# Mirror sums and differences, a narrower band and split pool weights in a two-layer mixer on one core

## The chip, the cores and the metric

The kernel runs on one core of one Trainium2 chip. The metric is the device time of one execution in microseconds (us), as a median of several runs. TensorE (PE) multiplies matrices, VectorE (DVE) and ScalarE (ACT) work on elements, SyncE (SP) issues the DMAs; GpSimd (POOL) does next to nothing here. Each engine takes its instructions in one fixed order. A matmul result lies in PSUM, everything else in SBUF.

## The reference

256 latent and 256 context tokens of width 2048 pass through two layers. In each layer one input projection feeds three mixers: attention, a mean over windows minus the token itself ("pool"), and the real part of a 2-D Fourier transform. The mixers' outputs are concatenated, multiplied by a gate and projected back. The last layer needs only keys and values of the context.

```
def multiscale_pool(u, pool_w, pool_scale):        # windows 2, 4, 8, 16, one for each of 4 groups
    ...
        outs.append(win_sum / cnt[None, :, None] - uf[:, :, gi])
    y = jnp.einsum('bngc,gcd->bngd', pooled, pool_w).reshape(B, N, POOL_W)
    return y * pool_scale

def fourier_mix(u, fourier_w):                     # 4 groups of 128 channels
    ...
    f = jnp.fft.fft2(uf, axes=(1, 3), norm='ortho').real.astype(u.dtype)
    return jnp.einsum('bngc,gcd->bngd', f, fourier_w).reshape(B, N, FOURIER_W)

def reference(...):
    for l in range(DEPTH):
        shift, scale, gate = jnp.split(jax.nn.silu(c) @ ada_w[l] + ada_b[l], 3, axis=-1)
        h = rmsnorm(x, norm_g[l]) * (1.0 + scale[:, None]) + shift[:, None]
        q, k, v, up, uf, g = split_proj(h @ w_in[l])
        ...
        out = merge_branches(att, up, uf, g, pool_w[l], pool_scale[l], fourier_w[l], w_out[l])
        x_new = x + gate[:, None] * out
        ...  # the same for the context tokens, except in the last layer
    return rmsnorm(x, final_norm_g)
```

## The kernel before

**Products in two parts.** Nearly every product is kept near full precision by splitting both operands into a high and a low part, each of a reduced type (fp32r). `mm3` (L336 to L338) issues three matmuls: high by high, high by low, low by high. `split` makes the parts: ScalarE copies with rounding to the high part (L138), DVE subtracts that from the source for the low part (L139).

**Weights.** `wpiece` loads 128x1024 pieces (`raw`) and splits them into `whi` and `wlo`, with three buffers of each. They are used once, so ScalarE and DVE split each weight piece of the kernel while PE multiplies the piece before.

**Stages of a layer.** `b_chunk` computes 512 columns of the input projection for all tokens: 4 token tiles of 128 in layer 0 (latent and context), 2 in layer 1 (latent). Chunk 0 holds the pool channels, chunk 1 the Fourier channels, chunk 2 the keys and values. Then follow gates, queries, attention and the output projection. After chunks 0 and 1, `evac_tok` splits the token-major result into high and low parts (`u`).

**Pool branch.** For each of four groups a first product with a band matrix of 256x256 (L359, token tile by token tile) gives z, which ScalarE copies to SBUF (L364). The second product with the 128x128 pool weights is one matmul of full-precision operands (L347), and DVE writes it scaled (L349).

**Fourier branch.** The channel transform and the Fourier weights are folded into one table `fh`, `fl` per layer (L404, L406, L407). For each group the first product multiplies both token tiles of a sequence by 256 columns of cosines and sines (`dh`, `dl`): six matmuls per sequence. z is split by `split`, and the second product multiplies it by `fh`, `fl`, 130 columns for the cosine half and 128 for the sine half. DVE writes the mirror halves of the output as sum and difference (L428, L429).

**What sets the order.** Branches are generators. While PE runs a chunk, `side.tick(0.64)` advances a clock, and a branch takes its next step when the clock passes what it asked for (`yield`, in us, and a lag). LAG_E and the numbers at the yields thus decide between which weight products a step's matmuls stand. `fill(n)` adds n units of adaLN work for later stages: one 512 KB load (`araw`) and two products on DVE with an accumulated sum (`ajunk`, L189) against a broadcast of c (`cbt`). The broadcast has one buffer, reloaded when the unit list passes to another half of c. These units have low priority, weights and evacuations a high one (AHEAD). A scheduler then puts each engine's instructions into one order, in which they wait for each other.

**PSUM.** Chunk results use four tiles (`mm`), the branches four others (`sm`).

Of the kernel before, what the change touches and what calls it, by code (L numbers as in the profile page):

```python
# [28 lines left out]
WINDOWS = (2, 4, 8, 16)  # L29

# [15 lines left out]
LEAD = 3  # L46
LAG_S, LAG_T, LAG_E, LAG_Q = 4.3, 1.4, 5.6, 0.0
# [3 lines left out]
FILL = ((1.69, 1.5, 0.55, 1.43, 1.0), (0.04, 1.61, 0.01, 0.66, 0))  # L51
# [4 lines left out]
def backbone(  # L56
# [270 lines left out]

    def pair8(n, rest):
        q8 = late["q8"]
        if n == 4:  # L330
            return [q8.tile([P, n, *rest], F32R, tag="q8", name=name("q8")) for _ in range(2)]
        t = q8.tile([P, 2, n, *rest], F32R, tag="q8", name=name("q8"))
        return t[:, 0], t[:, 1]
# [6 lines left out]
    def pool_branch(l, u, mixed, off, nst):  # L340
# [4 lines left out]
        def second(g, zs):  # L345
            y = smt()
            PE.matmul(y[:, :nt], pwt[:, g], zs, start=True, stop=True)  # L347
            for s in range(nst):
                V.scalar_tensor_tensor(  # L349
                    mixed[2][:, g, off + s * N : off + s * N + N], y[:, s * N : s * N + N], psc[:, l * 4 + g : l * 4 + g + 1], it[:, g],  # L350
                    op0=ALU.mult, op1=ALU.mult,
                )

        for g in range(4):
            z = smt()
            for s in range(nst):
                for mt in range(2):
                    for i in range(2):
                        PE.matmul(  # L359
                            z[:, s * N : s * N + N], u[i][:, 2 * s + mt, g * P : g * P + P], br[g][:, mt],  # L360
                            start=mt == 0 and i == 0, stop=mt == 1 and i == 1,
                        )
            zs = t2("z", (P, nt))
            S.copy(zs, z[:, :nt])  # L364
# [10 lines left out]
    def pool_tables(l):  # L375
        pwt = t2("pw", (P, 4, P))
        nc.sync.dma_start(pwt, pw[l])
        it = f4("icnt", (P, 4, N), F32)
# [9 lines left out]
        tabs.update(p=(pwt, it, br))  # L388
# [21 lines left out]
    def fourier_branch(l, u, mixed, off, nst):  # L410
# [20 lines left out]
        for g in range(4):  # L431
            c = slice(g * P, g * P + P)
            z = smt()
            for s in range(nst):
                for mt in range(2):
                    mm3(z[:, s * N : s * N + N], u[0][:, 2 * s + mt, c], u[1][:, 2 * s + mt, c], dh[:, mt], dl[:, mt], mt == 0, mt == 1)
            zh, zl = t2("zh", (P, 512), F32R), t2("zl", (P, 512), F32R)
            split(z[:, :nt], zh[:, :nt], zl[:, :nt])
            yield 0.72 * nst, 1.3
# [131 lines left out]
    def layer(l, h, xs, chunk0):  # L571
# [35 lines left out]
        u = evac_tok(accs, ntt)  # L607
# [4 lines left out]
        side.add("four", fourier_branch(l, u, mixed, off, nst), LAG_E)  # L612
# [437 lines left out]
def _order():  # L1050
    h = N // 2
    return np.concatenate([np.arange(h + 1), N - np.arange(1, h)])


def _tables():
# [12 lines left out]
    ang = 2 * np.pi * (np.outer(t, t) % N) / N  # L1068
    d = np.concatenate([np.cos(ang), np.sin(ang)], 1).astype(np.float32)
    dft = d.reshape(2, P, 512).transpose(1, 0, 2)  # L1070
    dft0 = np.concatenate([dft[:, :, : N // 2 + 1], dft[:, :, N + 1 : N + N // 2]], 2)
# [80 lines left out]
```

## Time and profile before

| | us |
|---|---|
| median of 3 runs (1077.66 to 1080.66) | 1078.14 |
| profiled execution | 1079.1 |
| its span in the trace | 1077.2 |
| PE busy | 1045.6 |
| DVE busy | 846.3 |
| ACT busy | 480.5 |

The conditioning for layer 0 is made first, from large loads; from then on PE has work nearly throughout. Matmuls are pipelined: the duration of one in the trace overlaps the next, so what a matmul costs is read from start to start. DVE's rows are shorter from start to start than they are long, too. A row with a bracket says how long the engine was idle before it, and what ended that.

### The profile page before, as it was taken

The numbers are of one execution on the slowest core, as the hardware profiler recorded it, in microseconds if no ns is written. First come the engines' busy times: TensorE is split into PE (matmuls) and PEld (weight loads), VectorE is DVE, ScalarE is ACT, GpSimd is POOL, SyncE is SP. The second block draws the span as 40 slices with busy tenths as digits, with TensorE's granted clock in tenths as the row PEclk, the third lists the DMA queues.
The fourth block names the chain that finished last, engine by engine and source line by source line (L and its number), as shares of the span: only waits on it lengthen the run. The fifth ranks groups of instructions, "written<-read, shape, count | busy, mean of one in ns | idle before, by whom it ended". The sixth has DMA issues, their size and how long they took to land.

```text
span 1077.2 us, 14001 instructions
## 1 busy us (share of the span) xinstructions
PE 1045.6 (97%) x5065; PEld 842.2 (78%) x5065; DVE 846.3 (79%) x1566; ACT 480.5 (45%) x807; POOL 0.2 (0%) x4
## 2 busy tenths in 40 slices
PE   5999899999999999999999999999999999999996
PEld 3466577788787888888888888888888888888885
DVE  6458656998999879997999887589656888776564
ACT  5233234323413765642532223288326768547443
POOL 0000000000000000000000000000000000000000
PEclk9999999999999999999999999999999999999998
DMA  9999857457685334457786657435765565776563
GB/s 355 414 368 345 277 200 239 157 190 233 200 266 195 96 122 155 157 195 259 251 286 218 198 195 262 139 127 190 246 229 170 159 195 184 236 262 215 180 213 115
DMA packets 64133, 234.15 MB, mean 217 GB/s; under 512 B 7153, under 2 KB 8257, under 8 KB 60353
## 3 DMA queue, kind: packets, MB, share of 16 engines
q1 hardware_dynamic: 64064, 233.28, 63.4%
q8 instruction: 39, 0.64, 0.3%
q14 instruction: 30, 0.24, 0.1%
HBM read 231.12 MB, written 2.12 MB: 217 GB/s over the span
## 4 chain that ended last, share of the span: by engine, by line
PE 66%; DVE 6%; issue 3%; ACT 1%; DMA 1%; ACTq 0%; SPq 0%; DVEq 0%
PE mm L336 17%; PE mm L338 17%; PE mm L337 17%; PE mm L312 5%; DVE ajunk L189 3%; PE mm L313 2%; PE sm L337 2%; PE sm L336 2%; PE sm L338 2%; DVE wlo L139 1%; PE sm L557 1%; DMA cbt<-cd 1%; PE sm L520 1%; DMA araw<-in_adar 0%; ACT whi L138 0%
## 5 line engine op out<-in xcount | busy, mean ns | idle before, releaser
L138 ACT CAST whi<-raw 128x1024 fp32r<-128x1024 f32 (+1 forms) x216 | 219.9, 1019 | 333.5 <-PE mm L338 108.5
L139 DVE TENSOR_TENSOR wlo<-raw,whi 128x1024 fp32r<-128x1024 f32 (+1 forms) x216 | 255.1, 1182 | 104.4 <-ACT whi L138 103.2
L189 DVE SCALAR_TENSOR_TENSOR ajunk<-araw,cbt 128x1024 bf16<-128x1024 f32 x224 | 273.6, 1221 | 48.5 <-DMA araw<-in_adar 35.2
L336 PE MATMUL mm<-whi,h 128*128 128x512 f32 x416 | 167.5, 403 | 0.0
L337 PE MATMUL mm<-wlo,h 128*128 128x512 f32 x416 | 162.8, 391 | 0.0
L338 PE MATMUL mm<-whi,h 128*128 128x512 f32 x416 | 162.8, 391 | 0.0
L336 PE MATMUL mm<-m,whi 128*128 128x512 f32 (+1 forms) x272 | 102.7, 377 | 0.0
L338 PE MATMUL mm<-m,wlo 128*128 128x512 f32 (+1 forms) x272 | 102.5, 377 | 0.0
L337 PE MATMUL mm<-m,whi 128*128 128x512 f32 (+1 forms) x272 | 102.5, 377 | 0.0
L312 PE MATMUL mm<-h,whi 128*128 128x512 f32 x256 | 92.5, 401 | 0.0
L338 PEld LDWEIGHTS mm<-whi,h 128*128 128x128 f32 x416 | 78.1, 188 | 16.9 <-DVE h L139 0.3
L337 PEld LDWEIGHTS mm<-wlo,h 128*128 128x128 f32 x416 | 78.3, 188 | 15.6 <-issue 1.4
L336 PEld LDWEIGHTS mm<-whi,h 128*128 128x128 f32 x416 | 78.3, 188 | 15.7 <-issue 1.4
L336 PE MATMUL mm<-h,whi 128*128 128x512 f32 x196 | 77.8, 397 | 0.2 <-DVE vl L139 0.2
L338 PE MATMUL mm<-h,wlo 128*128 128x512 f32 x196 | 76.8, 392 | 0.0
L337 PE MATMUL mm<-h,whi 128*128 128x512 f32 x196 | 76.7, 391 | 0.0
L313 PE MATMUL mm<-h,wlo 128*128 128x256 f32 x256 | 72.4, 283 | 0.0
L915 PE MATMUL mm<-whi,h 128*128 128x512 f32 x192 | 65.8, 413 | 1.9 <-ACT h L138 1.9
L337 PEld LDWEIGHTS mm<-m,whi 128*128 128x128 f32 x272 | 51.2, 188 | 9.5
L338 PEld LDWEIGHTS mm<-m,wlo 128*128 128x128 f32 x272 | 51.2, 188 | 9.4
L336 PEld LDWEIGHTS mm<-m,whi 128*128 128x128 f32 x272 | 51.2, 188 | 9.3
L312 PEld LDWEIGHTS mm<-h,whi 128*128 128x128 f32 x256 | 48.2, 188 | 10.8
(224 smaller groups left out, 1641.1 us busy)
## 6 DMA issues: line engine op xcount, KB each, us to landing
araw<-in_adar SPq DMA_DIRECT2D x128, 512.0 KB, 4.0
raw<-in_wb SPq DMA_DIRECT2D x78, 512.0 KB, 3.8
raw<-in_wg SPq DMA_DIRECT2D x55, 512.0 KB, 4.1
a<-in_ada SPq DMA_DIRECT2D x24, 1024.0 KB, 7.7
raw<-in_wo SPq DMA_DIRECT2D x32, 512.0 KB, 4.4
raw<-in_wot SPq DMA_DIRECT2D x32, 512.0 KB, 3.5
a<-in_ada SPq DMA_DIRECT2D x16, 512.0 KB, 5.4
x<-in_xT SPq DMA_DIRECT2D x4, 1024.0 KB, 7.5
```

Of the source, the lines that this page charges most:

```text
L138: i = S.copy(hi, src)
L139: V.tensor_sub(lo, src, hi.bitcast(F32))
L189: V.scalar_tensor_tensor(junk, raw, 1.0, cbt[:, v], op0=ALU.mult, op1=ALU.mult, accum_out=acc[:, u, h, v : v + 1])
L312: PE.matmul(a.rearrange("p (s n) -> p s n", s=2), hi[:, j - j0], h.both[k][:, :, :N], start=s0, stop=False)
L313: PE.matmul(a[:, :N], lo[:, j - j0], h.hi[k][:, :N], start=False, stop=s1)
L336: PE.matmul(o, ah, bh, start=start, stop=False)
L337: PE.matmul(o, ah, bl, start=False, stop=False)
L338: PE.matmul(o, al, bh, start=False, stop=stop)
L520: PE.transpose(tp[:, hh * P : hh * P + P], qo[:, hh], idt)
L557: PE.transpose(tp[:, h * P : h * P + P], ps[h][:, i * P : i * P + P], idt)
L915: PE.matmul(o, lt, r, start=s0, stop=s1)
```

## The change

Four things are changed.

1. The latent and context tokens come in another order: the even tokens of the first half, then the odd ones, then the mirror token of each. `evac_fold` takes the place of `evac_tok` for the Fourier branch: DVE makes the sum and the difference of each pair of mirror tokens from the two token tiles (in layer 1 ScalarE copies one of them to SBUF first) and splits both. The first product then needs fewer columns: per group and sequence one matmul of 256 columns and two of 192 for the differences, three of 130 for the sums.
2. The second token tile's band product covers only the columns from BAND0 on, where the band is not zero: 128, 130, 194 and 196 columns for the four windows.
3. Pool weights and pool z are split in high and low parts. The second product of the pool is `mm3`, three matmuls.
4. The Fourier branch starts after a lag of 4.6 times the number of sequences instead of 5.6, its first step asks for 0.46 instead of 0.72 per sequence, and the FILL numbers of layer 0 change: 1.69 to 1.4 per piece of chunk 1, 1.5 to 1.35 in chunk 2, 1.0 to 1.08 in the output projection.

```diff
--- before.py
+++ after.py
@@ -27,6 +27,7 @@
 NH = 8
 EPS = 1e-6
 WINDOWS = (2, 4, 8, 16)
+BAND0 = (128, 126, 62, 60)
 
 AHEAD = 400
 ST = 4
@@ -44,11 +45,12 @@
 TJ = 2
 T2 = 11
 LEAD = 3
+LAG_F = 4.6
 LAG_S, LAG_T, LAG_E, LAG_Q = 4.3, 1.4, 5.6, 0.0
 GROUPS = (1, 1, 2, 2, 2, 2, 2, 2, 1, 1)
 LOW = -400
 PRE = 6
-FILL = ((1.69, 1.5, 0.55, 1.43, 1.0), (0.04, 1.61, 0.01, 0.66, 0))
+FILL = ((1.4, 1.35, 0.55, 1.43, 1.08), (0.04, 1.61, 0.01, 0.66, 0))
 VB, VG, VF, VS, VC, VW = 0, 96, 128, 144, 152, 184
 
 
@@ -325,6 +327,21 @@
                 split(accs[tt], hi[:, tt], lo[:, tt])
         return hi, lo
 
+    def evac_fold(accs, nst):
+        hi, lo = pair8(2 * nst, (512,))
+        with tc.high_priority(offset=AHEAD):
+            for s in range(nst):
+                a, b = accs[2 * s], accs[2 * s + 1]
+                if nst == 1:
+                    b = t2("mir")
+                    S.copy(b, accs[1])
+                e, o = t2("ev"), t2("od")
+                V.tensor_add(e, a, b)
+                split(e, hi[:, 2 * s], lo[:, 2 * s])
+                V.tensor_sub(o, a, b)
+                split(o, hi[:, 2 * s + 1], lo[:, 2 * s + 1])
+        return hi, lo
+
     def pair8(n, rest):
         q8 = late["q8"]
         if n == 4:
@@ -344,7 +361,7 @@
 
         def second(g, zs):
             y = smt()
-            PE.matmul(y[:, :nt], pwt[:, g], zs, start=True, stop=True)
+            mm3(y[:, :nt], pwt[0][:, g], pwt[1][:, g], *zs)
             for s in range(nst):
                 V.scalar_tensor_tensor(
                     mixed[2][:, g, off + s * N : off + s * N + N], y[:, s * N : s * N + N], psc[:, l * 4 + g : l * 4 + g + 1], it[:, g],
@@ -357,11 +374,12 @@
                 for mt in range(2):
                     for i in range(2):
                         PE.matmul(
-                            z[:, s * N : s * N + N], u[i][:, 2 * s + mt, g * P : g * P + P], br[g][:, mt],
+                            z[:, s * N + (mt and BAND0[g]) : s * N + N], u[i][:, 2 * s + mt, g * P : g * P + P],
+                            br[g][:, mt, mt and BAND0[g] :],
                             start=mt == 0 and i == 0, stop=mt == 1 and i == 1,
                         )
-            zs = t2("z", (P, nt))
-            S.copy(zs, z[:, :nt])
+            zs = t2("zh", (P, nt), F32R), t2("zl", (P, nt), F32R)
+            split(z[:, :nt], *zs)
             yield 0.43 * nst, 1.0
             if prev:
                 second(*prev)
@@ -375,6 +393,8 @@
     def pool_tables(l):
         pwt = t2("pw", (P, 4, P))
         nc.sync.dma_start(pwt, pw[l])
+        ph, pl = t2("ph", (P, 4, P), F32R), t2("pl", (P, 4, P), F32R)
+        split(pwt, ph, pl)
         it = f4("icnt", (P, 4, N), F32)
         nc.sync.dma_start(it, icnt)
         br = []
@@ -385,7 +405,7 @@
                 b2 = f4("bandr", (P, 2, 2, N))
             br.append(b2[:, g % 2])
             S.copy(br[g], bt)
-        tabs.update(p=(pwt, it, br))
+        tabs.update(p=((ph, pl), it, br))
 
     def fourier_tables(l):
         fwt = t2("fw", (P, 512))
@@ -432,11 +452,16 @@
             c = slice(g * P, g * P + P)
             z = smt()
             for s in range(nst):
-                for mt in range(2):
-                    mm3(z[:, s * N : s * N + N], u[0][:, 2 * s + mt, c], u[1][:, 2 * s + mt, c], dh[:, mt], dl[:, mt], mt == 0, mt == 1)
+                zs = z[:, s * N : s * N + N]
+                oh, ol = (x[:, 2 * s + 1, c] for x in u)
+                PE.matmul(zs, oh, dh[:, 1], start=True, stop=False)
+                PE.matmul(zs[:, P // 2 :], oh, dl[:, 1, P // 2 :], start=False, stop=False)
+                PE.matmul(zs[:, P // 2 :], ol, dh[:, 1, P // 2 :], start=False, stop=False)
+                w = slice(0, P + 2)
+                mm3(zs[:, w], u[0][:, 2 * s, c], u[1][:, 2 * s, c], dh[:, 0, w], dl[:, 0, w], False, True)
             zh, zl = t2("zh", (P, 512), F32R), t2("zl", (P, 512), F32R)
             split(z[:, :nt], zh[:, :nt], zl[:, :nt])
-            yield 0.72 * nst, 1.3
+            yield 0.46 * nst, 1.3
             if prev:
                 second(*prev)
                 yield 0.36 * nst, 0.5
@@ -604,12 +629,12 @@
                 for tt in range(ntt):
                     V.tensor_add(part[:, tt], part[:, tt], accs[tt])
             accs = [part[:, tt] for tt in range(ntt)]
-        u = evac_tok(accs, ntt)
+        u = evac_fold(accs, nst)
         if l == 0:
             mixed[1] = ap_.tile([P, 4, T], F32, tag="A1", name=name("mix"))
         if l == 1:
             list(mc)
-        side.add("four", fourier_branch(l, u, mixed, off, nst), LAG_E)
+        side.add("four", fourier_branch(l, u, mixed, off, nst), LAG_F * nst)
         accs = b_chunk(l, 2, h, 4, FILL[l][1])
         side.finish("four")
         kT = f4("kh", (P, 2, T)), f4("kl", (P, 2, T))
@@ -1048,8 +1073,8 @@
 
 
 def _order():
-    h = N // 2
-    return np.concatenate([np.arange(h + 1), N - np.arange(1, h)])
+    t0 = np.concatenate([np.arange(0, N // 2, 2), np.arange(1, N // 2, 2)])
+    return np.concatenate([t0, [N // 2], N - t0[1:]])
 
 
 def _tables():
@@ -1065,10 +1090,12 @@
         m[np.arange(N), np.arange(N)] -= cnt
         band[gi] = m.reshape(2, P, N).transpose(1, 0, 2)
         icnt[:, gi] = (1.0 / cnt)[None]
-    ang = 2 * np.pi * (np.outer(t, t) % N) / N
-    d = np.concatenate([np.cos(ang), np.sin(ang)], 1).astype(np.float32)
-    dft = d.reshape(2, P, 512).transpose(1, 0, 2)
-    dft0 = np.concatenate([dft[:, :, : N // 2 + 1], dft[:, :, N + 1 : N + N // 2]], 2)
+    ang = 2 * np.pi * (np.outer(t[:P], t[: P + 1]) % N) / N
+    dft0 = np.zeros((P, 2, N), np.float32)
+    dft0[1:, 0, : P + 1] = np.cos(ang)[1:]
+    dft0[0, 0, : P + 1] = t[: P + 1] % 2 == 0
+    dft0[0, 1, :P] = t[:P] % 2
+    dft0[1:, 1, P + 1 :] = np.sin(ang)[1:, 1:P]
     e = np.arange(P)
     an = 2 * np.pi * (np.outer(e, e) % P) / P
     cc = np.stack([np.cos(an), -np.sin(an)], 1).astype(np.float32)
```

All later lines move: L138/L139 are now L140/L141, L189 is L191, L336 to L338 are L353 to L355, L349 is L366, L407 is L427, L428/L429 are L448/L449.

How the change moves instructions is shown at three places of DVE's order. A row is line, operation, output, inputs and size.

The first is layer 0's pool branch, at its last groups, before: `wlo` is the low part of a weight, L349 writes the pool's output, L407 the low part of the Fourier table.

```order
L407 SCALAR_TENSOR_TENSOR fl_1469<-sm_1470,fh_1468 128x512
L407 SCALAR_TENSOR_TENSOR fl_1469<-sm_1477,fh_1468 128x512
L139 TENSOR_TENSOR wlo_1710<-raw_1707,whi_1709 128x1024
L349 SCALAR_TENSOR_TENSOR mix_1425<-sm_1608,vt,icnt_1254 128x256 x2
L349 SCALAR_TENSOR_TENSOR mix_1425<-sm_1615,vt,icnt_1254 128x256 x2
L595 SCALAR_TENSOR_TENSOR mix_1425<-mix_1425,th_1440 128x512
```

And after, where `zl` is the low part of the pool's z:

```order
L427 SCALAR_TENSOR_TENSOR fl_1473<-sm_1474,fh_1472 128x512
L427 SCALAR_TENSOR_TENSOR fl_1473<-sm_1481,fh_1472 128x512
L141 TENSOR_TENSOR wlo_1732<-raw_1729,whi_1731 128x1024
L141 TENSOR_TENSOR zl_1597<-sm_1587,zh_1596 128x512
L366 SCALAR_TENSOR_TENSOR mix_1429<-sm_1618,vt,icnt_1258 128x256 x2
L366 SCALAR_TENSOR_TENSOR mix_1429<-sm_1627,vt,icnt_1258 128x256 x2
```

The last z of the pool has a low part now, and it stands behind a weight's low part.

The second is layer 0's Fourier branch, from the low part of group 2's z to that of group 3, before:

```order
L139 TENSOR_TENSOR zl_1840<-sm_1826,zh_1839 128x512
L189 SCALAR_TENSOR_TENSOR ajunk_1645,acc<-araw_1643,cbt_1386 128x1024
L428 TENSOR_TENSOR mix_1426<-sm_1864,w_1872 128x2x127
L429 TENSOR_TENSOR mix_1426<-sm_1864,w_1872 128x2x127
L189 SCALAR_TENSOR_TENSOR ajunk_1647,acc<-araw_1643,cbt_1386 128x1024
L139 TENSOR_TENSOR zl_1894<-sm_1880,zh_1893 128x512
```

And after:

```order
L141 TENSOR_TENSOR zl_1892<-sm_1878,zh_1891 128x512
L191 SCALAR_TENSOR_TENSOR ajunk_1814,acc<-araw_1812,cbt_1390 128x1024
L141 TENSOR_TENSOR wlo_2047<-raw_2044,whi_2046 128x1024
L448 TENSOR_TENSOR mix_1430<-sm_1916,w_1924 128x2x127
L449 TENSOR_TENSOR mix_1430<-sm_1916,w_1924 128x2x127
L191 SCALAR_TENSOR_TENSOR ajunk_1816,acc<-araw_1812,cbt_1390 128x1024
L191 SCALAR_TENSOR_TENSOR ajunk_1820,acc<-araw_1818,cbt_1390 128x1024
L141 TENSOR_TENSOR zl_1946<-sm_1932,zh_1945 128x512
```

Between the two low parts stand a weight's low part and one adaLN product more.

The third is the same place in layer 1, before:

```order
L139 TENSOR_TENSOR zl_6626<-sm_6618,zh_6625 128x256
L189 SCALAR_TENSOR_TENSOR ajunk_6791,acc<-araw_6789,cbt_4437 128x1024
L428 TENSOR_TENSOR x_965_4660<-sm_6652,w_6660 128x127
L429 TENSOR_TENSOR x_965_4660<-sm_6652,w_6660 128x127
L139 TENSOR_TENSOR zl_6676<-sm_6668,zh_6675 128x256
```

And after:

```order
L141 TENSOR_TENSOR zl_6677<-sm_6669,zh_6676 128x256
L141 TENSOR_TENSOR wlo_6816<-raw_6813,whi_6815 128x1024
L448 TENSOR_TENSOR x_969_4676<-sm_6703,w_6711 128x127
L449 TENSOR_TENSOR x_969_4676<-sm_6703,w_6711 128x127
L191 SCALAR_TENSOR_TENSOR ajunk_6845,acc<-araw_6843,cbt_4530 128x1024
L141 TENSOR_TENSOR zl_6727<-sm_6719,zh_6726 128x256
```

A weight's low part has moved in between, from a place ahead of group 2's.

## Rows read from the trace of the kernel before

**Rows 1.** Page, part 1: busy us (share of the span) x instructions, by engine.

```profile
PE 1045.6 (97%) x5065; PEld 842.2 (78%) x5065; DVE 846.3 (79%) x1566; ACT 480.5 (45%) x807; POOL 0.2 (0%) x4
```

**Rows 2.** Table of stretches: length, busy (x instructions) by engine, PEclk, DMA share, GB/s.

```profile
215.00:262.00 47.00, 46.84 (x240) 39.85 (x239) 41.10 (x67) 13.33 (x28) 0.00 (x0) 1.00 0.64 212
```

**Rows 3.** PE timeline, layer 1 Fourier: start us, us, engine, operation, [idle before].

```profile
774.86 0.39 PE L338 MATMUL mm<-whi,h 128*128 128x512 f32 x1
775.09 0.22 PE L336 MATMUL sm<-zh,fh 128*128 128x130 f32 x1
...
775.99 0.39 PE L337 MATMUL mm<-wlo,h 128*128 128x512 f32 x1
776.22 0.39 PE L338 MATMUL mm<-whi,h 128*128 128x512 f32 x1
776.45 0.28 PE L336 MATMUL sm<-dd,q 128*128 128x256 f32 x1
...
777.39 0.40 PE L337 MATMUL mm<-wlo,h 128*128 128x512 f32 x1
```

**Rows 4.** PE timeline, layer 0, around a second pool product.

```profile
188.83 0.40 PE L338 MATMUL mm<-whi,h 128*128 128x512 f32 x1
189.06 1.02 PE L347 MATMUL sm<-z,pw 128*128 128x512 f32 x2
...
190.15 0.40 PE L337 MATMUL mm<-wlo,h 128*128 128x512 f32 x1
```

**Rows 5.** DVE timeline, layer 0, pool to the last Fourier group.

```profile
190.12 0.88 DVE L349 SCALAR_TENSOR_TENSOR mix<-sm,vt,icnt 128x256 f32<-128x256 f32 x2 [1.47 <-PE sm L347]
...
216.17 1.22 DVE L139 TENSOR_TENSOR wlo<-raw,whi 128x1024 fp32r<-128x1024 f32 x1
217.31 0.68 DVE L139 TENSOR_TENSOR zl<-sm,zh 128x512 fp32r<-128x512 f32 x1
217.91 1.21 DVE L189 SCALAR_TENSOR_TENSOR ajunk<-araw,cbt 128x1024 bf16<-128x1024 f32 x1
...
219.16 1.23 DVE L189 SCALAR_TENSOR_TENSOR ajunk<-araw,cbt 128x1024 bf16<-128x1024 f32 x1
...
230.53 0.69 DVE L139 TENSOR_TENSOR zl<-sm,zh 128x512 fp32r<-128x512 f32 x1 [0.26 <-ACT zh L138]
```

**Rows 6.** ACT timeline, layer 0, copy of the first pool product.

```profile
187.38 0.59 ACT L364 COPY z<-sm 128x512 f32<-128x512 f32 x1 [4.53 <-PE sm L359]
```

**Rows 7.** PE timeline, layer 0, second product of the last Fourier group.

```profile
233.20 0.28 PE L336 MATMUL sm<-zh,fh 128*128 128x260 f32 x1
```

**Rows 8.** PE's waits: line <- releaser: us in total, times, longest.

```profile
PE sm L520 <- DVE nt L236: 1.0, 1, 1.0
...
PE mm L336 <- DVE vl L139: 0.2, 1, 0.2
```

**Rows 9.** DVE timeline, layer 0, reload of the broadcast and v.

```profile
246.91 1.22 DVE L139 TENSOR_TENSOR wlo<-raw,whi 128x1024 fp32r<-128x1024 f32 x1
252.65 1.23 DVE L189 SCALAR_TENSOR_TENSOR ajunk<-araw,cbt 128x1024 bf16<-128x1024 f32 x1 [4.52 <-issue]
...
261.01 0.42 DVE L139 TENSOR_TENSOR vl<-mm,vh 128x256 fp32r<-128x256 f32 x1
```

**Rows 10.** DVE timeline, layer 1, low parts of Fourier groups 2 and 3.

```profile
778.60 0.42 DVE L139 TENSOR_TENSOR zl<-sm,zh 128x256 fp32r<-128x256 f32 x1
...
780.47 0.41 DVE L139 TENSOR_TENSOR zl<-sm,zh 128x256 fp32r<-128x256 f32 x1
```

**Rows 11.** PE timeline, startup, its longest wait for DVE's sums.

```profile
133.59 0.65 PE L964 MATMUL sm<-a,cs 128*32 128x256 f32 x4 [4.38 <-DVE red L998]
```

**Rows 12.** Table of stretches, startup, that wait and what follows.

```profile
130.00:135.00 5.00, 1.41 (x9) 0.60 (x10) 4.02 (x13) 0.00 (x0) 0.00 (x0) 0.68 0.80 296
135.00:140.00 5.00, 5.00 (x20) 2.99 (x20) 2.76 (x9) 1.06 (x3) 0.00 (x0) 0.64 0.75 280
```

## Prediction

> **What bounds the kernel now.** I read the page's table of engines first: TensorE (PE) is busy for 97% of the span and VectorE (DVE) for 79% [rows 1]. So work taken off PE should shorten the kernel by its own length, as long as no other engine makes PE wait. The shares are averages, so the table of stretches comes next: while layer 0's Fourier branch runs, PE is busy for 46.84 of 47.00 us and DVE for 41.10 [rows 2]. DVE has 13% of slack there, and the changed branch gives it more to do. PE's list of waits is third: behind layer 0's start only single waits of a microsecond or less are left, among them 1.0 us for the norm before the head transposes and 0.2 us for the low part of v [rows 8]. The timelines then give the prices.
>
> **What PE saves.** In layer 1 six Fourier products of 128 or 130 columns lie between the 512-column rows that start at 774.86 and 775.99: 1.13 us. Six of 256 columns lie between 776.22 and 777.39: 1.17 us [rows 3]. Both intervals hold the same two 512-column issues, 0.23 each (775.99 to 776.22), so six narrow ones take 0.67 and six wide ones 0.71: 0.112 against 0.119 each. Halving the columns saves 7 ns of 119. The page "TensorE: Matmul & The Clock Gate" of the Trainium skill, section "LDWEIGHTS (loading the stationary operand)", puts a load of 128 stationary columns at columns / 1.2, an estimated 107 ns whatever the moving width; the 112 ns of the narrow rows agree with that rule. By it narrowing would gain nothing, and PE's sum below would be 0.55 us smaller.
>
> - First Fourier product: per group and sequence still six matmuls, widths 256, 192, 192 and three of 130 in place of six of 256. Narrowed: 5 x 4 groups x 3 sequences (two in layer 0, one in layer 1) = 60, at most 7 ns each: -0.4 us.
> - Band products: the second token tile narrows to 128, 130, 194 or 196 columns. 2 x 4 x 3 = 24, at most 7 ns: -0.15.
> - Second pool product: one full-precision matmul becomes three. Before, 188.83 to 190.15 holds it and two 512-column issues [rows 4]: 1.32 - 0.46 = 0.86. After: 3 x 0.23 = 0.69. -0.17 x 4 = -0.7 in layer 0; half the width in layer 1, so about half: -0.35.
>
> Sum on PE: **-1.6 us**. That is nearly all that the change takes away; no weight byte and no 512-column product goes.
>
> **What DVE gets.** One 128x512 operation costs 0.60 to the next start (217.31 to 217.91), a weight's low part 1.14 (216.17 to 217.31), an adaLN product 1.25 before another (217.91 to 219.16) [rows 5] and less before other work; I take 1.2. New in layer 0: the pool weights' low part, four pool low parts, four sums and differences: 9 x 0.60 = 5.4 us. In layer 1 four pool low parts are half as wide: 0.6 + 4 x 0.42 (the 256-column row at 261.01 [rows 9]) + 2 x 0.6 = 3.5. The high parts replace copies that ScalarE made already, except for the pool weights' and the mirror copy of layer 1, and ScalarE is far from full. FILL takes about 4 x 0.29 + 8 x 0.15 = 2.4 adaLN units out of chunks 1 and 2, two products each: 4.7 x 1.2 = 5.7 us, given back in the output projection, where I cost it at nothing (if that cover failed, 5.7 us of DVE work would show as waits there). On average, then, DVE breaks even. What counts is where its queue stands when PE needs a result.
>
> **Layer 0, last Fourier group: +4.0 us.** The Fourier products of group 3 need the low part of its z. In the DVE order the first pool product's low part and that Fourier low part are 60 rows apart. Before, the stretch from the first pool evacuation at 190.12 to that low part at 230.53 took 40.4 us [rows 5] and held 16 adaLN products, 5 weight low parts and 16 operations of 512 columns, beside four pool evacuations and four rows of mixing. After, between those two points stand 22, 6 and 24, and the same rest: +6 x 1.2 + 1.14 + 8 x 0.60 = +13.1, so 53.5; before held 0.9 us of idle in four pieces (one is the 0.26 at 230.53), of which a fuller queue keeps some: 52.6 to 53.5, I take 52.9. The stretch starts when the first pool z has been copied, 187.38 + 0.59 = 188.0 [rows 6]. The low part then starts at 240.9 and is there at 241.5 or a little later. PE reached this point at 233.20 before [rows 7], 2 us after the low part was done. After, 157 instead of 139 rows of 512 columns stand ahead of it from the first pool z on, because the side clock gives the branch a longer lag (9.2 for 5.6): +18 x 0.23 = 4.1; the second pool products give 0.7 and the narrow rows 0.35 back: 236.3. Two small waits come on the way. PE reaches the last pool group's second product before its low part, which stands behind a weight's low part in DVE's order: +0.6. And z tiles of PSUM come free only after DVE's low part, where ScalarE's copy alone freed them: +0.7. So PE is there at 237.6 and waits until 241.5: **+4.0**. Bounds: 0, as DVE was 2 us early here before and the count leaves out what PE itself may lose on the way, and 6, if each of the 22 products takes the dearer 1.25 (+1.1) and all the idle stays (+0.6).
>
> **After chunk 2: +1.0 us.** The broadcast of c is replaced there: DVE's row at 252.65 stands 4.52 us for its issue, and the low part of v starts at 261.01 [rows 9], 0.2 us late [rows 8]. Between reload and low part stood 5 products, after it is 7 (+2.4, less about 0.4 of a second wait for the reload). The last product with the old broadcast ends at about 250.0 (241.5, five products, one weight part, four mixing rows) where it was about 247: +3.0. So the low part is due 5.0 later, and PE 3.8 later (4.0 + 1.3 of waits - 1.5 of work): 1.2 late in place of 0.2. Bounds 0 and 2.5.
>
> **Layer 1, last Fourier group: +1.1 us.** Before, the low parts of groups 2 and 3 start 1.87 us apart, 778.60 and 780.47 [rows 10]. After, a weight's low part (1.14) stands between them as well, and PE has as little work between their uses as before. Bounds 0 and 1.2: the araw loads make DVE idle just before, so it may run ahead.
>
> **Given back: -0.6 us.** Before the head transposes PE waits 1.0 us for DVE [rows 8]; in the new DVE order one rotation product of 512 columns stands behind the rotated sum and no longer ahead of it: -0.60. Bounds 0 and -1.0. Startup's order changes (bands and pool weights are loaded and cast earlier) I cost at nothing: the first Fourier table still waits for a load behind the same weights; bounds -1 and +1.
>
> **Sum:** -1.6 + 0.6 + 0.7 + 4.0 + 1.0 + 1.1 - 0.6 = +5.2 on the profiled execution's 1079.1, which lies 0.96 above the median of 1078.14. So +5.2 on the median: 1083.3; rounded down a little, as the bounds of the small waits reach to zero more easily than up: **1083.0 us**.
>
> **Rivals.**
> 1. DVE keeps up. Its queue drains through the waits that it has now (0.9 us of idle in the stretch, and 2 us of margin at 233.20), the adaLN products that FILL took away leave just the room that the low parts need, and PE's saving shows: 1078.1 - 1.6, and 0.6 given back as above: 1075.9, no difference. For it: on average DVE's work in these chunks does not grow (5.4 in, 5.7 out). Against: the count of rows up to the low part does.
> 2. Width counts. If a matmul cost in proportion to its columns, 130 for 256 would save 0.059 and 192 half of that: 36 x 0.059 + 24 x 0.030 in the Fourier branch and 12 x 0.059 + 12 x 0.030 in the bands, 3.9 us in place of 0.55, and with DVE on time the sum would be -1.05 - 3.9 - 0.6 = -5.6: 1072.5, faster. Against: the 0.112 of [rows 3]. The Trainium skill's page "TensorE: Matmul & The Clock Gate", section "Back-to-back issue gap", tables 134 cycles for 128 columns and 262 for 256, nearly half, for a matmul by itself; the spacings in [rows 3] contradict it for this stream, where each matmul loads its own weights.
> 3. The wait drops the clock. The one wait of this length in the trace, 4.38 us before 133.59 [rows 11], is followed by granted clocks of 0.68 and 0.64 in the next two stretches of 5 us [rows 12], so part of each ran at 1.2 and not 2.4 GHz. At the Fourier branch PE has no slack: two stretches at 0.66 lose 0.34 x 5 x 2 = 3.4 us at the most, half that if part of the stretch was the wait itself: 1084.8 to 1086.5, slower. The point that decides is a wait of about 4 us; it is on the edge.
> 4. Only the small waits come (0.6, 0.7 and 1.0, less 0.6), not the two of the last Fourier groups: -1.6 + 1.7 = +0.1, 1078.2, no difference.
>
> **How the numbers follow.** About 0.3% (3.2 us) is what a measurement of this kernel tells from no change: faster is below 1074.9, slower above 1081.4. Forecast 0.42; clock drop 0.16; DVE keeps up 0.19; small terms only 0.15; width counts or another gain 0.08. Slower: 0.42 + 0.16 = 0.58; same 0.34; faster 0.08. The range leaves out the width rival and the far end of the clock rival: 1075.5 to 1087.0. The forecast's own is 1081.5 to 1085.
>
> **What would show it.** A row of PE on the low part of z of layer 0's last Fourier group with about 4 us idle before it, released by DVE; the v row with 1.2; narrow rows of 192 and 130 columns at 0.115 or 0.112 from start to start; the three pool rows 0.69 long together; PE's busy time 1.6 us less. If PE has no wait over 1 us there, the forecast is wrong and rival 1 or 4 holds; if narrow rows stand 0.06 apart, rival 2.

## The result and the profile after

The changed kernel took 1087.34 us (median of 6 runs, 1086.63 to 1092.62), the kernel before 1078.51: a ratio of 1.0087 (95% interval 1.0069 to 1.0105). It is slower by 7 to 11 us; 1083.0 was forecast, with a range to 1087.0. The direction held, the size did not. The profiled execution took 1087.53 us, 8.4 more than that of before, with a span of 1085.4.

First the page's table of engines, after:

```profile
PE 1049.1 (97%) x5073; PEld 842.7 (78%) x5073; DVE 855.5 (79%) x1582; ACT 482.7 (44%) x810; POOL 0.2 (0%) x4
```

PE's busy time rose by 3.5 us [rows 1], where 1.6 less was forecast: matmuls became slower somewhere. DVE's rose by 9.2.

The same steps of PE in both kernels show where the time was lost: the Fourier table, the first gate product of layer 0, the first product of its output projection, the first head transposes of layer 1, and the last matmul. Columns are those of [rows 3]. Before:

```profile
184.44 0.67 PE L404 MATMUL sm<-fw,cct 128*128 128x512 f32 x1 [1.56 <-DMA cct<-in_cc]
...
287.99 0.39 PE L336 MATMUL mm<-whi,h 128*128 128x512 f32 x1
...
533.39 0.39 PE L336 MATMUL mm<-m,whi 128*128 128x512 f32 x1
...
823.81 0.27 PE L508 MATMUL sm<-idt,qo 128*128 128x128 f32 x1
...
1068.03 0.39 PE L338 MATMUL mm<-whi,m 128*128 128x512 f32 x1
```

And after:

```profile
184.74 0.67 PE L424 MATMUL sm<-fw,cct 128*128 128x512 f32 x1 [1.32 <-DMA cct<-in_cc]
...
292.51 0.39 PE L353 MATMUL mm<-whi,h 128*128 128x512 f32 x1
...
539.70 0.39 PE L353 MATMUL mm<-m,whi 128*128 128x512 f32 x1
...
831.23 0.27 PE L533 MATMUL sm<-idt,qo 128*128 128x128 f32 x1
...
1076.21 0.39 PE L355 MATMUL mm<-whi,m 128*128 128x512 f32 x1
```

PE is 0.30 us later at the Fourier table, 4.52 at the gates, 6.31 at the output projection, 7.42 at layer 1's head transposes and 8.18 at the end. So 4.2 us were lost from layer 0's pool branch to its gates, 1.8 in its gates and attention, 1.1 in the first half of layer 1 and 0.8 in its attention.

**The Fourier branch.** DVE's end of its queue there, after (it answers to [rows 5]):

```profile
188.22 0.69 DVE L141 TENSOR_TENSOR zl<-sm,zh 128x512 fp32r<-128x512 f32 x1 [0.31 <-ACT zh L140]
...
236.61 1.22 DVE L141 TENSOR_TENSOR wlo<-raw,whi 128x1024 fp32r<-128x1024 f32 x1
...
238.41 1.22 DVE L191 SCALAR_TENSOR_TENSOR ajunk<-araw,cbt 128x1024 bf16<-128x1024 f32 x1
...
239.67 1.23 DVE L191 SCALAR_TENSOR_TENSOR ajunk<-araw,cbt 128x1024 bf16<-128x1024 f32 x1
...
240.82 0.69 DVE L141 TENSOR_TENSOR zl<-sm,zh 128x512 fp32r<-128x512 f32 x1
```

The stretch began at 188.22 and the low part of the last group at 240.82, where 188.0 and 240.9 were forecast. PE at the same place:

```profile
237.39 0.39 PE L355 MATMUL mm<-whi,h 128*128 128x512 f32 x1
238.64 0.36 PE L353 MATMUL sm<-zh,fh 128*128 128x260 f32 x1 [0.86 <-DVE mix L449]
241.56 0.39 PE L354 MATMUL sm<-zl,fh 128*128 128x260 f32 x1 [2.56 <-DVE zl L141]
...
242.50 0.63 PE L353 MATMUL mm<-whi,h 128*128 128x512 f32 x1
242.93 0.63 PE L354 MATMUL mm<-wlo,h 128*128 128x512 f32 x1
...
245.06 0.55 PE L353 MATMUL mm<-whi,h 128*128 128x512 f32 x1
245.45 0.39 PE L354 MATMUL mm<-wlo,h 128*128 128x512 f32 x1
```

PE had come to this product at 237.62 (237.39 and one issue); 237.6 was forecast. It waited until 241.56: 0.86 for the row of mixing that frees a PSUM tile, then 2.56 for the low part, ahead of which two adaLN products stand behind that row (238.41 and 239.67). After the wait 512-column products start 0.43 us apart (242.50 to 242.93) until 245.06, where 0.23 is the rule. The table of stretches shows why, in the column that reads 0.70 and 0.96:

```profile
240.00:245.00 5.00, 3.44 (x11) 2.93 (x12) 4.97 (x10) 0.54 (x2) 0.00 (x0) 0.70 0.56 186
245.00:250.00 5.00, 5.00 (x22) 4.08 (x21) 4.80 (x9) 1.05 (x1) 0.00 (x0) 0.96 0.44 138
```

That column is the granted clock: part of this time ran at 1.2 instead of 2.4 GHz. It cost (1 - 0.70) x 5 + (1 - 0.96) x 5 = 1.7 us, and PE's rows from 241.56 to 245.45 are as much longer than the same rows at full clock. So rival 3 did not stand against the forecast, it came on top of it.

**Behind it.** The other waits of PE that are new or longer, after: the pool's low part, attention in layer 0, a pool product and the last attention block in layer 1.

```profile
200.61 0.50 PE L354 MATMUL sm<-zl,ph 128*128 128x512 f32 x1 [0.38 <-DVE zl L141]
...
349.58 0.30 PE L545 MATMUL sm<-idt,qo 128*128 128x128 f32 x1 [0.67 <-DVE nt L238]
...
399.63 0.33 PE L582 MATMUL sm<-idt,p 128*128 128x128 f32 x1 [0.51 <-ACT p L565]
...
750.18 0.38 PE L376 MATMUL sm<-bandr,q 128*128 128x256 f32 x1 [0.53 <-DVE zl L141]
...
919.20 0.33 PE L582 MATMUL sm<-idt,p 128*128 128x128 f32 x1 [1.70 <-ACT p L570]
```

Behind the last of them stands DVE again. ScalarE's operation needed the reciprocal of a sum (L569), which stood behind an adaLN product and a weight's low part, and DVE had waited for the load of that adaLN product:

```profile
915.88 1.23 DVE L191 SCALAR_TENSOR_TENSOR ajunk<-araw,cbt 128x1024 bf16<-128x1024 f32 x1 [2.24 <-DMA araw<-in_adar]
...
917.03 1.22 DVE L141 TENSOR_TENSOR wlo<-raw,whi 128x1024 fp32r<-128x1024 f32 x1
918.17 0.16 DVE L569 RECIPROCAL nm<-nm 128x1 f32<-128x1 f32 x1
```

The low part of v started when it was expected to, near 266.0:

```profile
266.17 0.42 DVE L141 TENSOR_TENSOR vl<-mm,vh 128x256 fp32r<-128x256 f32 x1
```

But PE came to it only afterwards:

```profile
267.01 0.39 PE L353 MATMUL mm<-h,whi 128*128 128x512 f32 x1
```

PE was 1.7 us later than forecast because of the clock, so the wait of 1.2 that I had counted there was not seen.

**Prices.** Three pool products of layer 0 take 0.68 us (189.29 to 189.97), as worked out:

```profile
189.29 0.39 PE L353 MATMUL sm<-zh,ph 128*128 128x512 f32 x1
...
189.97 0.39 PE L353 MATMUL mm<-whi,h 128*128 128x512 f32 x1
```

Twelve narrow Fourier products, after, and the two 512-column issues behind them:

```profile
232.73 0.32 PE L457 MATMUL sm<-dd,q 128*128 128x256 f32 x1
...
234.07 0.45 PE L353 MATMUL mm<-whi,h 128*128 128x512 f32 x1
234.35 0.39 PE L354 MATMUL mm<-wlo,h 128*128 128x512 f32 x1
```

They take 1.34 us, and the issue behind them is 0.05 longer than usual (0.28). The same twelve at 256 columns in the first experiment:

```profile
231.75 0.28 PE L457 MATMUL sm<-dd,q 128*128 128x256 f32 x1
...
233.18 0.40 PE L353 MATMUL mm<-whi,h 128*128 128x512 f32 x1
233.41 0.40 PE L354 MATMUL mm<-wlo,h 128*128 128x512 f32 x1
```

1.43 us, then 0.23. So narrowing gives 0.04 us here. This group gives the least: the other three of layer 0 take 1.30 or 1.31 us where experiment 1 takes 1.42 to 1.44, with the same 0.05 behind them. Over the four groups 0.28 us are saved by 40 narrowed products, 7 ns each, as I had taken.

### The profile page after: what moved, and what is told of

It is laid out like the page before. It is cut to its first block, busy times and chain, and to the rows that moved or that the text cites. A ratio compares the mean times of both kernels' runs of the same rounds, so it can differ in the third digit from the quotient of the medians.

```text
span 1085.4 us, 14049 instructions
## 1 busy us (share of the span) xinstructions
PE 1049.1 (97%) x5073; PEld 842.7 (78%) x5073; DVE 855.5 (79%) x1582; ACT 482.7 (44%) x810; POOL 0.2 (0%) x4
## 3 DMA queue, kind: packets, MB, share of 16 engines
HBM read 231.12 MB, written 2.12 MB: 215 GB/s over the span
## 4 chain that ended last, share of the span: by engine, by line
PE 79%; DVE 7%; DMA 6%; ACT 5%; issue 3%; SPq 0%; ACTq 0%; DVEq 0%
PE mm L355 17%; PE mm L353 17%; PE mm L354 17%; PE mm L940 6%; PE mm L314 5%; PE sm L940 4%; DMA araw<-in_adar 2%; PE mm L315 2%; PE sm L989 2%; DVE ajunk L191 2%; DVE wlo L141 2%; ACT whi L140 2%; PE sm L354 2%; PE sm L353 2%; PE sm L355 2%
## 5 line engine op out<-in xcount | busy, mean ns | idle before, releaser
L140 ACT CAST whi<-raw 128x1024 fp32r<-128x1024 f32 (+1 forms) x216 | 219.9, 1019 | 312.6 <-PE mm L355 112.6
L141 DVE TENSOR_TENSOR wlo<-raw,whi 128x1024 fp32r<-128x1024 f32 (+1 forms) x216 | 255.1, 1182 | 103.2 <-ACT whi L140 102.1
L191 DVE SCALAR_TENSOR_TENSOR ajunk<-araw,cbt 128x1024 bf16<-128x1024 f32 x224 | 273.6, 1222 | 52.3 <-DMA araw<-in_adar 39.9
L353 PE MATMUL mm<-whi,h 128*128 128x512 f32 x416 | 166.0, 399 | 0.0
L355 PE MATMUL mm<-whi,h 128*128 128x512 f32 x416 | 163.4, 393 | 0.0
L353 PE MATMUL mm<-m,whi 128*128 128x512 f32 (+1 forms) x272 | 102.6, 377 | 0.0
L355 PE MATMUL mm<-m,wlo 128*128 128x512 f32 (+1 forms) x272 | 102.4, 376 | 0.0
L355 PEld LDWEIGHTS mm<-whi,h 128*128 128x128 f32 x416 | 78.4, 188 | 16.7 <-DVE h L141 0.3
L353 PEld LDWEIGHTS mm<-whi,h 128*128 128x128 f32 x416 | 78.7, 189 | 14.9 <-issue 0.5
L353 PE MATMUL mm<-h,whi 128*128 128x512 f32 x196 | 77.7, 396 | 0.0
L355 PE MATMUL mm<-h,wlo 128*128 128x512 f32 x196 | 76.7, 391 | 0.0
L355 PEld LDWEIGHTS mm<-m,wlo 128*128 128x128 f32 x272 | 51.2, 188 | 9.4
L353 PEld LDWEIGHTS mm<-m,whi 128*128 128x128 f32 x272 | 51.2, 188 | 9.3
```

Source lines behind the costliest of these rows:

```text
L140: i = S.copy(hi, src)
L141: V.tensor_sub(lo, src, hi.bitcast(F32))
L191: V.scalar_tensor_tensor(junk, raw, 1.0, cbt[:, v], op0=ALU.mult, op1=ALU.mult, accum_out=acc[:, u, h, v : v + 1])
L353: PE.matmul(o, ah, bh, start=start, stop=False)
L355: PE.matmul(o, al, bh, start=False, stop=stop)
```

## The experiments

Three theories. **Queue:** the adaLN products that the order puts ahead of the low parts make PE wait, and the clock falls behind the wait. "The stretch" is DVE's from the first pool evacuation (or the first pool low part, where there is one) to the low part of layer 0's last Fourier group. The kernel before was timed again beside each group of experiments (medians of 1077.17 to 1077.54), so kernels of different groups are compared by their ratios. **Work:** the added operations of DVE cost their time, wherever they stand. **Numbers:** the new lag and FILL values cost it. All kernels compute the whole result.

### 1 and 2: the same products at full width

```diff
-PE.matmul(zs[:, P // 2 :], oh, dl[:, 1, P // 2 :], ...)
-PE.matmul(zs[:, P // 2 :], ol, dh[:, 1, P // 2 :], ...)
-w = slice(0, P + 2)
+PE.matmul(zs, oh, dl[:, 1], ...)
+PE.matmul(zs, ol, dh[:, 1], ...)
+w = slice(0, N)
-PE.matmul(z[:, s * N + (mt and BAND0[g]) : s * N + N], ..., br[g][:, mt, mt and BAND0[g] :], ...)
+PE.matmul(z[:, s * N : s * N + N], ..., br[g][:, mt], ...)   # experiment 1 only
```

> The changed kernel with every Fourier and band product at its full 256 columns (the table is zero where the changed kernel leaves columns out). Queue theory: the adaLN products that stand ahead of the low part of layer 0's last Fourier group make PE wait, and the clock falls after it. In the order of this kernel 16 of them stand in the stretch in place of 22, so DVE is done at about 234 and PE arrives at 237: no wait there, no fall of the clock. 0.9 + 2.6 + 1.7 us come back, 0.5 us of column work is added: about 1082.6 us (1081 to 1084). Work theory: the sums, differences and low parts themselves cost the time, wherever they stand: 1087.8. Width theory (narrow matmuls cost in proportion to columns): 1087.3 + 3.9 = 1091.

> The changed kernel with only the Fourier products at 256 columns, the band products narrow. Its order has 17 adaLN products in the stretch. Queue theory: the low part is there at 235, PE at 237: no wait, clock at 1.00, about 1082.5 us, the same as with both at full width. If the band's width mattered by itself, this kernel would differ from the one with both wide by more than 1 us. Work theory: 1087.7.

Both at full width: 1079.62 us, ratio 1.0020 (1.0010 to 1.0030). Only Fourier wide: 1081.60, ratio 1.0036 (1.0022 to 1.0051). More columns, the same sums, splits and schedule numbers, and with both at full width the ratio fell from 1.0087 to 1.0020: about 7 of the 9 us were gone. In the first kernel DVE's low part of the last group, and then PE's use of it:

```profile
234.05 0.69 DVE L141 TENSOR_TENSOR zl<-sm,zh 128x512 fp32r<-128x512 f32 x1
```

```profile
236.67 0.28 PE L353 MATMUL sm<-zh,fh 128*128 128x260 f32 x1
236.79 0.29 PE L354 MATMUL sm<-zl,fh 128*128 128x260 f32 x1
```

The low part was done at 234.7 and PE came at 236.79: no wait. The 5 us around it and the 5 us after:

```profile
235.00:240.00 5.00, 5.00 (x29) 4.35 (x28) 4.67 (x10) 2.04 (x5) 0.00 (x0) 1.00 0.68 209
240.00:245.00 5.00, 5.00 (x24) 4.14 (x23) 4.81 (x7) 0.66 (x2) 0.00 (x0) 1.00 0.47 139
```

The clock stayed at 1.00. Work is refuted: DVE did the same work (854.9 us busy against 855.5). The queue theory had the place right, but gave back too little in experiment 1 (1082.6 expected, 1081 to 1084): the waits at the pool's low parts (195.15, 200.61, 750.18 in the changed kernel) went too. In experiment 2, with the band narrow, they were still there, and the last attention block waited longer, 2.12 us, with the clock falling behind it:

```profile
912.25 0.33 PE L582 MATMUL sm<-idt,p 128*128 128x128 f32 x1 [2.12 <-ACT p L570]
```

```profile
910.00:915.00 5.00, 2.88 (x13) 2.41 (x12) 3.84 (x9) 2.45 (x5) 0.00 (x0) 0.78 0.31 108
915.00:920.00 5.00, 5.00 (x28) 4.23 (x27) 4.17 (x6) 2.58 (x6) 0.00 (x0) 0.87 0.63 185
```

That fall is worth (0.22 + 0.13) x 5 = 1.75 us, about as much as the whole difference between the two kernels, whose intervals touch. So an effect of the band's width on the time is not shown. Layer 0's two waits at the pool's low parts do go with it: they stand in experiments 2, 3, 4 and 10, where the band is narrow, and neither in 1 nor in 12, where it is wide.

### 3: the schedule numbers of before

```diff
-FILL = ((1.4, 1.35, 0.55, 1.43, 1.08), ...
+FILL = ((1.69, 1.5, 0.55, 1.43, 1.0), ...
-            yield 0.46 * nst, 1.3
+            yield 0.72 * nst, 1.3
-        side.add("four", ..., LAG_F * nst)
+        side.add("four", ..., LAG_E)
```

> The changed kernel with the lag, the step's claim and the FILL numbers of before. PE comes to the last Fourier group 4 us earlier (139 rows of 512 columns in place of 157) and the low part at 237 in place of 241, with 20 adaLN products ahead of it. Queue theory: the wait is 4.5 to 5 us, as long as before or longer, and the clock falls: 1087 to 1089 us. If the new schedule numbers were the cause (rival), the time falls to 1079 to 1082.

1084.85 us, ratio 1.0074 (1.0059 to 1.0090): less than expected, not told apart from the changed kernel (1.0069 to 1.0105), and far from before. The wait stood at the same product, shorter than the 4.5 to 5 us expected, as the low part started at 235.72:

```profile
236.46 0.58 PE L354 MATMUL sm<-zl,fh 128*128 128x260 f32 x1 [3.83 <-DVE zl L141]
```

The granted clock fell to 0.51 and 0.80 in the stretches of 5 us from 235 on. So the new numbers are not needed for the loss: with the old ones PE came earlier, and the low part, with 20 adaLN products ahead of it, still came after PE.

### 4: no fill in chunks 1 and 2

```diff
-FILL = ((1.4, 1.35, 0.55, 1.43, 1.08), ...
+FILL = ((0, 0, 0.55, 1.43, 1.8), ...
```

> The changed kernel with FILL 0 for chunks 1 and 2 of layer 0 and 1.8 in the output projection, so that only 7 adaLN products stand in the stretch. Queue theory: the low part is there at 223, PE at 237: no wait at the last Fourier group and none for pool's low part, 1081.5 us (1080 to 1084), if the units given back later hide there. Work theory: the waits stay, 1087. If the units do not hide in the output projection, PE waits there for low parts of weights: up to 15 x 1.2 = 18 us more.

1103.72 us, ratio 1.0246 (1.0231 to 1.0261). The waits at the last Fourier group were gone. Two things that I expected did not come: the low part started at 234.64 and not near 223, as DVE now stood idle for 10.9 us of the stretch, and the pool's waits stayed (0.22 at 194.88, 0.37 at 200.34), so the adaLN products do not make those. The time is 26 us above before, lost elsewhere. The adaLN units did not hide in the output projection, and PE stood before layer 1 for what they feed:

```profile
732.53 0.79 PE L353 MATMUL mm<-whi,h 128*128 128x512 f32 x1 [14.56 <-ACT h L140]
```

The theories are told apart by the place, not by this time.

### 5, 6, 7 and 8: one part at a time

Experiment 5 is the kernel before with the pool change alone, 6 with the narrow band alone, 7 with the schedule numbers alone. Experiment 8 is experiment 1 with the old pool product: new token order, sums and differences, schedule numbers. The edit of 5:

```diff
-            PE.matmul(y[:, :nt], pwt[:, g], zs, start=True, stop=True)
+            mm3(y[:, :nt], pwt[0][:, g], pwt[1][:, g], *zs)
-            S.copy(zs, z[:, :nt])
+            split(z[:, :nt], *zs)
```

> The kernel before with only the pool change: weights and z in two parts, three fast matmuls for the second product. By the term of the forecast PE saves 0.7 + 0.35 us; the order keeps 16 adaLN products in the stretch, low part at 231, PE at 233: no wait at the Fourier branch. Queue theory: 1076.3 us (1075.5 to 1077.5), a ratio of 0.999. Work theory (each DVE operation that is added costs its time on the path): 5 + 2 us of low parts more, 1080 to 1083.

> The kernel before with only the band products narrowed. PE work changes by -0.15 us at most. The order has 18 adaLN products in the stretch in place of 16: low part at 232.7, PE at 233.1. Queue theory: no wait or a few tenths, 1077.3 (1076.5 to 1078.5). If narrowing the band costs time by itself, as the 2 us between the kernel with both wide and the one with only the Fourier products wide hint: 1079.

> The kernel before with only the lag, the step's claim and the FILL numbers of the changed kernel. PE comes to the last Fourier group at 237, the low part is there at 235 (19 adaLN products): no wait. Queue theory: 1077.5 (1076.5 to 1079). If the schedule numbers cost by themselves: above 1080.

> The changed kernel with the old pool branch and all Fourier and band products at 256 columns: what is left is the new token order, the sums and differences and the schedule numbers. 17 adaLN products in the stretch, low part at 234.8, PE at 237.2. Queue theory: no wait at the Fourier branch, 1080.5 us (the 1079.6 of the wide kernel plus the pool's 1.05). Work theory: 8 sum and difference operations less 0, about the same as the wide kernel less 5 us of low parts: 1075 to 1077.

| | median us | ratio to before (95% interval) |
|---|---|---|
| 5, pool | 1076.79 | 0.9996 (0.9987 to 1.0004) |
| 6, band narrow | 1079.14 | 1.0008 (0.9998 to 1.0018) |
| 7, schedule numbers | 1076.69 | 0.9998 (0.9986 to 1.0010) |
| 8, fold at full width | 1077.98 | 1.0005 (0.9996 to 1.0014) |

Each interval holds no difference from before. For 5 and 7 the queue theory gave this; 6 came out above its number, but with an interval that holds no change; 8 came 2.5 us lower than the queue theory's sum and above the work theory's. No part costs 8 us by itself, also not the five operations of 512 columns that the pool adds to DVE in layer 0.

### 9 and 12: narrow Fourier products without the pool change, and with a wide band

Experiment 9 is the changed kernel with the diff of experiment 5 undone, 12 the changed kernel with the band at full width.

> The changed kernel with the old second product and the old copy of the pool; narrow Fourier and band products, fold and schedule numbers stay. The order has 23 adaLN products in the stretch, one more than the changed kernel: low part at 242.4, PE at 237.5. Queue theory: about 4.5 us of wait and the fall of the clock stay, 1087 us (1085.5 to 1088.5). If the pool's four low parts made the queue long (work theory), the wait shrinks by 4 x 0.6 = 2.4 us, the clock stays up and the time is 1082 to 1084.

> The changed kernel with only the band products at full width; the Fourier products stay narrow. 21 adaLN products in the stretch: low part at 240.3, PE at 237.6. Queue theory: a wait of about 2.7 us and some fall of the clock stay, 1085.5 us (1084 to 1087). If the two narrowings count alike, it is where the kernel with only the Fourier products wide is, 1081.6.

1084.56 us, ratio 1.0068 (1.0052 to 1.0085), and 1085.08, ratio 1.0066 (1.0046 to 1.0085). The time of 9 lies between the ranges of the two theories, that of 12 in the range of the queue theory; the rows tell them apart. With the pool's low parts gone, the wait at the last Fourier group was still there in 9:

```profile
237.39 0.36 PE L353 MATMUL sm<-zh,fh 128*128 128x260 f32 x1 [1.35 <-DVE mix L447]
240.31 0.58 PE L354 MATMUL sm<-zl,fh 128*128 128x260 f32 x1 [2.56 <-DVE zl L141]
```

1.35 and 2.56 us, longer than in the changed kernel (0.86 and 2.56), and the clock fell too (0.86 and 0.50 from 235 to 245). Kernel 12 waited 1.34 and 2.56 at the same rows, more than the 2.7 expected, with the clock at 0.66 from 240 to 245; it also waited 1.49 at a Fourier product of layer 1 (783.10), and the clock fell to 0.85 and 0.81 there. With experiments 1 and 2 this fills a square: both narrow 1.0087, only Fourier narrow 1.0066, only the band narrow 1.0036, both wide 1.0020. The Fourier widths are worth about 5 us each way, with intervals clear of each other. The band's 2 us are within the intervals in both pairs.

### 10: narrow products, but fewer adaLN products in the queue

```diff
-FILL = ((1.4, 1.35, 0.55, 1.43, 1.08), ...
+FILL = ((0.5, 0.5, 0.9, 1.43, 1.2), ...
```

> The changed kernel, all narrow, with FILL of layer 0 at 0.5, 0.5, 0.9, 1.43 and 1.2: about ten units of adaLN work go from chunks 1 and 2 to the query chunks and the output projection, and 17 products stand in the stretch in place of 22. Queue theory: the low part is there at 235.4, PE at 237: no wait at the last Fourier group and the clock at 1.00, so 5 us less there: 1082 us (1080.5 to 1084), if the moved units hide. Work theory or a cost of the narrow products themselves: the wait stays, 1087. If the units are late for layer 1's conditioning, a wait before layer 1 says so.

1082.73 us, ratio 1.0046 (1.0029 to 1.0063), in the expected range. The wait shrank from 3.4 to 0.67 us, and the granted clock stayed at 1.00 in the stretches from 235 to 250:

```profile
236.89 0.39 PE L354 MATMUL sm<-zl,fh 128*128 128x260 f32 x1 [0.67 <-DVE zl L141]
```

This separates the columns from the queue: all products are narrow here, and the large wait is gone because 17 adaLN products stand in the stretch and not 22. The time does not reach experiment 1's. New waits stand in layer 1, the longest at a Fourier product:

```profile
778.08 0.36 PE L457 MATMUL sm<-dd,q 128*128 128x256 f32 x1 [1.44 <-DVE x L449]
```

There the clock fell as well:

```profile
775.00:780.00 5.00, 3.56 (x20) 2.89 (x19) 3.70 (x9) 0.85 (x4) 0.00 (x0) 0.88 0.35 115
780.00:785.00 5.00, 5.00 (x25) 4.19 (x25) 1.83 (x4) 0.86 (x4) 0.00 (x0) 0.78 0.62 213
```

The fall is worth (0.12 + 0.22) x 5 = 1.7 us, and with the wait that is about what experiment 10 lies above experiment 1. Experiment 12 waits at this product too, with FILL unchanged, so the moved units alone need not be the cause.

### 11: the two parts that did not lose, together

The kernel before with the pool change and the schedule numbers.

> The kernel before with the pool change and the new schedule numbers, without the fold and without narrow products. Low part at 234.1, PE at 236.5: no wait. Each part alone gave 0.4 to 0.5 us less than before; if PE's saving adds to it: 1076.3 us (1075 to 1077.5), a ratio of 0.999.

1077.48 us, ratio 0.9999 (0.9991 to 1.0008). No version beat the kernel before by more than can be told.

## Why the prediction was wrong

- **PE's saving of 1.6 us: right, but not seen in the time.** The pool product's 0.68 and the 7 ns of a narrow product came as counted. Experiment 5, which has only the pool's 1.05, came to 0.9996, with an interval that holds this saving as well as none.
- **The wait at the last Fourier group: right** in place, cause and size: low part at 240.82 (240.9 forecast), PE there at 237.62 (237.6), and 3.9 us lost against 4.0. That PE's arrival fits to 0.02 is partly luck: from start to start the two waits on the way cost 1.0 and not 1.3 (0.38 at 195.15, 0.65 at 200.61), and the Fourier table had come 0.30 later. With 16 adaLN products in the stretch (experiment 1) the wait was gone, with 17 (experiment 10) it was 0.67.
- **The step that failed first is the clock.** "At the Fourier branch PE has no slack ... it is on the edge": it was kept as a rival with a chance of 0.16 and left out of the sum. The trace of before had one wait of this length, 4.38 us, and the fall behind it [rows 11, 12]; that was the only evidence, and it pointed one way. That a wait of about 4 us decides was a guess from that one row; the runs have falls behind waits of 1.44 and 2.12 us as well. The fall cost 1.7 us here, and experiments 3, 9 and 12 have one at this place as well.
- **"After chunk 2: +1.0" did not come**, since PE had lost 1.7 us more on the way. DVE's part was right (266.17 for 266.0). Two waits of the kernel before went there too, 0.16 at 261.48 and 0.45 at 277.20.
- **"Given back: -0.6" was mis-sized.** The wait at 342.82 did shrink from 1.0 to 0.3, but a wait of 0.67 at 349.58 came in its place, and 0.74 at two rows of attention. From the gates to the output projection 1.8 us were lost where I had 0.6 gained, which is the largest miss in size. A wait costs more from start to start than its bracket says: the four waits cost 0.44 + 0.83 + 0.48 + 0.66 = 2.4 us, the one of before 1.1. So they account for 1.3 of the 1.8; 0.5 stays open.
- **Layer 1: +1.1 came, but not where I put it.** The last Fourier group did not wait; a pool product did for 0.53 (750.18), by the same mechanism as in layer 0 (a PSUM tile that waits for the low part), and a Fourier product for 0.17. The 1.70 at 919.20 in the last attention block was not in the sum; before it was 0.7. It follows the time that DVE stands idle for the load of the adaLN product ahead of the reciprocal: that idle time and PE's wait are 0.75 and 0.24 us in experiment 7, 1.25 and 0.73 before, 2.24 and 1.70 in the changed kernel, 2.62 and 2.12 in experiment 2: always about 0.5 apart. Experiment 9 has 0.23 and no wait. Why the load came later was not tried.
- **What I did not ask is why the queue was longer.** I read 22 adaLN products from the new order for 16 and gave no reason. The square shows that the narrow widths put them there: with the same work and the same numbers, 16 stand in the stretch at full width, 17 with only the Fourier products wide, 21 with only the band wide, and 22 at narrow. The order is made before the run, so its maker must have taken the widths into account; what it assumes of narrow products was not tried, and no run shows it. The price of a narrow product on PE was right to be nearly nothing; through DVE's order it was about 7 us.
- **Rivals.** 2 (width counts) is refuted by the spacings, 1 and 4 by the wait. The range ended at 1087.0 and was said to leave out "the far end of the clock rival", although that rival's own far end was 1086.5; the median was 0.34 beyond the range. The clock alone would have stayed inside it: the other terms, layer 0's attention above all, took the time out.

## What to carry to other kernels

When a program makes the engines' order, a change of shapes on one engine can reorder another. Count in the order what stands ahead of each result that a busy engine waits for; that count gave the low part's start here to 0.1 us. Where the sum already holds a wait as long as one that lowered the clock elsewhere in the trace, the clock belongs into the sum. And before a product is narrowed, compare two widths from start to start in the trace: where they cost the same, there is nothing to gain, only an order to lose.

## What the runs showed of the chip that was not expected

Single waits of PE shorter than the 4.38 us at startup were followed by a fall of the granted clock: 3.42 us in two pieces (0.70), 3.83 (0.51 and 0.80), 2.12 in the last attention block (0.78 and 0.87 in experiment 2), and even 1.44 and 1.49 at a Fourier product of layer 1 (0.88 and 0.78 in experiment 10, 0.85 and 0.81 in experiment 12). Longer ones were followed by 1.00: 1.75 us at 340.96 in experiment 1, and in the last attention block 1.70 (changed kernel) and 1.77 (experiment 12). So the length of one wait alone does not tell whether the clock falls; what does was not tried. Behind twelve narrow products the first 512-column product is followed 0.28 us later, not 0.23 (234.07 to 234.35, and 0.28 or 0.29 behind the other groups), so part of what narrow products save is given back behind them.
